# A state space branch rewritten: rotations on one engine, copies on two, 32-column output products

## The chip, the cores and the metric

The kernel runs on one core of one Trainium2 chip. The metric is the device time of one execution in microseconds (us). The core has five engines with a queue each: PE (TensorE, matrix products), DVE (VectorE), ACT (ScalarE), POOL (GpSimd) and SP, which here issues the weight transfers. Each works off its own queue in order and waits for the others by semaphores.

## What is computed

Two layers, 256 tokens of width 1024. Each layer is a feed-forward block, a mixer, and a second feed-forward block. The mixer projects the tokens to the input `u` of a state space branch, to an attention branch and to two gates, and adds up the gated branches:

```
h = rms_norm(x, norm_mix[l])
u, q_raw, k_cmp, ..., gate_a, gate_b = split(h @ w_in[l])
y_a = s5_branch(u, ...)              # 32 groups of 16 channels, 64 complex states each
y_b = nsa_branch(q_raw, ...) @ nsa_w_up[l]
x = x + (sigmoid(gate_a) * y_a + sigmoid(gate_b) * y_b) @ w_out[l]
```

and inside the state space branch

```
st[t] = abar * st[t-1] + bbar @ u[t]          (complex, per group)
y = gelu(Re(C st) + d * u)
val, gate = split(y @ w_glu); y_a = val * sigmoid(gate)
```

## The kernel before

**Weight stream and gemms.** All weights come as a stream of chunks. Each chunk is split into a rounded part on ACT (`whi`, line 156, or `hi` in line 318) and a rest on DVE (`wlo`, lines 157 and 318), with four buffers of each. A gemm multiplies two token tiles by four chunks: per k tile three products, lines 350 (`whi`, rounded activations), 351 (`whi`, their rest) and 352 (`wlo`), 512 columns each, 48 products in a gemm of `w_in`. The mixer's gemms follow each other: `u` (512 columns), keys and compressed values (384, then 408 columns), the compression products (line 488, 128x45), `q`, two gemms for each gate (called A0, A1, B0, B1 here), the GLU (four gemms), the up projection, the output.

**The state space branch** (`s5_main`) is a generator whose steps are issued between the chunks of these gemms. Four tokens make one chunk of the scan. Its steps: `U4`, 16 copies that put the four token phases of `uT` on four partition groups (u=0 on ACT, line 818; u=1 on DVE, line 820; u=2 and 3 on POOL through `gcopy`, line 480); 64 input products into banks `ya` and `yb` (line 488); a forward rotation by cos and sin (`rotate`; products on DVE, the additions of it on POOL in lines 881 and 885); two scans on DVE (line 838); a rotation back in two halves (half of the products, lines 882 and 883, and the subtraction of line 881 on POOL); the output products (line 488 once more) into `yb`: for each of 16 group pairs and each of three matrices (`K` on `U4`, two `C` on the states) two products of 64 output columns; and 32 gelus of 32x128 (line 857) that move the results from rows (token phase, channel) to rows of channels in `yt`, every fourth float of it at a time.

**Who stands near it.** On ACT, lines 1234 and 1236 (results of the 384 gemm, transposed by PE in line 1239), line 962 to 966 (408 gemm), line 1040 (gelu of the compressed keys `hid`, which needs `pb`, a one-column copy on DVE in line 1039), line 991 (the `q` gemm out of its bank) and 1264 (gates out of their banks). On DVE, lines 946 to 957 (rope of the keys) and 1008 to 1018 (of `q`), line 1048 (`kb`, which PE transposes in line 1055). The attention of each query tile goes by heads: scores on PE (line 1136), maximum on DVE, exponentials on ACT (1143), scaling on POOL (1159), transposes on PE (1169), copies on ACT (1171), products on PE (1180).

**What sets the order.** The instructions are written in the generator's order, but a scheduler in the build, with its own idea of durations, decides in which order each engine's queue gets them. So the change moves instructions that it doesn't name.

Of the kernel before, what the change touches and what calls it, by code (L numbers as in the profile page):

```python
# [24 lines left out]
# column offsets of the shape-only constants, packed side by side on 128 partitions  # L25
# [49 lines left out]
class Model:  # L75
# [31 lines left out]
    def add(k, ap, split=True, g=None):  # L107
        """g: (norm, first k tile) whose gains scale the rows"""
        k.chunks.append((ap, split, g))
# [65 lines left out]
    def next(k, la=None):  # L175
        """the next chunk of the stream; prepares later ones as far as buffers allow"""
        i = k.nu
        k.nu += 1
        if i and not k.chunks[i - 1][1]:
            k.held -= 1  # L180
        k.prepare(k.opt['LA'] if la is None else la)
        k.pull()
        return k.hl.pop(i)
# [132 lines left out]
    def split(k, src, hi, lo):  # L316
        """hi: src rounded to the product's type, lo: the rest"""
        return k.nc.scalar.copy(hi, src), k.nc.vector.tensor_sub(lo, src, hi.bitcast(F32))  # L318

    def rsqrt(k, ss, n, scale):  # L320
        """(ss*scale + eps)^-0.5 on [P, n]"""
# [13 lines left out]
    def norms(k):  # L335
        """1/rms of both token tiles, behind the weight preparation issued so far"""
# [3 lines left out]
    def transp4(k, src, t, half):  # L340
        """four 128x128 transposes of token-major src [128, 512] into hh/hl"""
# [12 lines left out]
    def finish(k, ys, sc, norm, parts):  # L354
        """x += sc * y and its transposed copy for the next phase. parts: the last products of token tile 0,
        and those of token tile 1 in two portions"""
# [24 lines left out]
    def gemm(k, stat, nk, cols, order=None, per=2, la=None):  # L381
        """two token tiles against the next weight chunks; returns the two banks.
        order: chunks per turn of a tile where the turns are to be kept"""
# [98 lines left out]
    def mm_cols(k, out, pairs, first, last=True):  # L482
        """sum of lhsT.T @ rhs over pairs, as two column tiles of the array that run side by side"""
# [8 lines left out]
    def s5_load(k, l):  # L492
        """DMAs of the S5 parameters of layer l"""
# [30 lines left out]
    def cmul(k, o, a, b, tmp, cost, M=None, conj=False):  # L524
        """(o0 + i o1) = (a0 +- i a1)(b0 + i b1), products on engine M; tmp(): scratch"""
# [18 lines left out]
    def s5_scalars(k):  # L544
# [31 lines left out]
        # angle to [-pi, pi]  # L576
# [19 lines left out]
        # expm1(a) = 2t/(1-t), cos-1 = -2 sin^2(th/2)  # L596
# [62 lines left out]
        # mag^4 and the unit rotation to the fourth power  # L659
# [11 lines left out]
    def s5_tables(k):  # L671
        """cos, sin of j*phi [128, 16, 64] and the decay of the scan"""
# [46 lines left out]
    def s5_mats(k):  # L719
# [7 lines left out]
        # powers times Bbar, dense: X[(g2 n), p, tau, c], tau = 3 - power  # L727
# [5 lines left out]
        # C transposed, pair-diagonal: CT[(g2 n), p, (g2' c)]  # L733
# [14 lines left out]
        # pair-diagonal copies, then the end-of-chunk input matrices  # L748
# [16 lines left out]
        # lag matrices: rows (tau, g2', c') hold lag 3 - tau  # L765
# [32 lines left out]
        # state-to-output matrices with abar^(s+1)  # L798
# [8 lines left out]
    def s5_main(k, uT):  # L807
        """uT [128 channels, 4, 256] -> yT hi/lo [128 channels, 4, 256]"""
# [4 lines left out]
        for q in range(4):  # L813
            for u in range(4):
                o = U4[u * 32:(u + 1) * 32].rearrange("p (a q) j -> p q a j", q=4)[:, q]
                i = uT[q * 32:(q + 1) * 32].rearrange("p a (j u) -> p u a j", u=4)[:, u]
                if u == 0:
                    S.copy(o, i)
                elif u == 1:
                    V.tensor_copy(o, i)  # L820
                else:
                    k.gcopy(o, i)
        yield 1.5
        yield 0.5
# [21 lines left out]
        yt = r4().rearrange("p (a t s) -> p a t s", a=4, s=4)  # L846
        for h in range(2):
            bk = k.bank((128, 8, 64), 'yb')
            for q in range(8):
                p = h * 8 + q  # L850
                k.mm_cols(bk[:, q], [(P['K'][:, p], U4[:, p]), (P['C'][0][:, p], Sp[0][:, p]),
                                     (P['C'][1][:, p], Sp[1][:, p])], q == 0)
# [522 lines left out]
```

## Time and profile before

| | |
|---|---|
| median of 3 runs | 1202.55 us (1201.87 to 1202.59) |
| span of the profiled execution | 1202.1 us |
| PE busy | 1162.6 us, 97% of the span |
| DVE / ACT / POOL busy | 844.5 / 687.7 / 251.4 us |
| PE idle between 220 and 350 us (first mixer), four longest waits | 5.3, 1.3, 1.2 and 0.5 us |
| the same between 810 and 940 us (second mixer) | 5.3, 1.2, 1.1 and 0.5 us |

An engine's busy time is the time covered by its instructions; PE's ends are modelled, and its products are pipelined, so what stands between two products is read from their starts. The span is a little shorter than the timed execution: the profiled one took 1202.1 us from first to last instruction, the median of the timed ones is 0.45 us longer. In a timeline row stand the start, the time covered, the engine, the line, the tiles written and read, the number of instructions merged, and in brackets the idle time ahead of it with the engine and line that ended it. An unqualified product of two f32 operands shows as two instructions, so 96 of them are 192 records.

### The profile page before, as it was taken

The numbers are of one execution on the slowest core, as the hardware profiler recorded it, in microseconds if no ns is written. First come the engines' busy times: TensorE is split into PE (matmuls) and PEld (weight loads), VectorE is DVE, ScalarE is ACT, GpSimd is POOL, SyncE is SP. The second block draws the span as 40 slices with busy tenths as digits, with TensorE's granted clock in tenths as the row PEclk, the third lists the DMA queues.
The fourth block names the chain that finished last, engine by engine and source line by source line (L and its number), as shares of the span: only waits on it lengthen the run. The fifth ranks groups of instructions, "written<-read, shape, count | busy, mean of one in ns | idle before, by whom it ended". The sixth has DMA issues, their size and how long they took to land. (4 is left out here: it accounts for less than half of the span.)

```text
span 1202.1 us, 18057 instructions
## 1 busy us (share of the span) xinstructions
PE 1162.6 (97%) x6326; PEld 947.3 (79%) x6326; DVE 844.5 (70%) x1466; ACT 687.7 (57%) x1228; POOL 251.4 (21%) x320
## 2 busy tenths in 40 slices
PE   7999999989999999999999999999899999999998
PEld 6888777877777888888888887778677778888886
DVE  5797979686865765555667987986967765655554
ACT  6655554738855565555566555555597645655552
POOL 3002654273212000000020053815532110000000
PEclk9999999999999999999999999999899999999999
DMA  7766555453543566656666656455635535666662
GB/s 234 220 182 186 166 156 183 116 158 112 178 126 98 175 210 185 186 182 187 189 183 183 196 160 181 140 155 147 193 89 158 132 117 172 210 179 189 192 183 80
DMA packets 150076, 200.44 MB, mean 167 GB/s; under 512 B 9952, under 2 KB 120832, under 8 KB 149984
## 3 DMA queue, kind: packets, MB, share of 16 engines
q1 hardware_dynamic: 148848, 197.46, 54.0%
q0 software_dynamic: 1136, 1.82, 0.9%
q8 instruction: 50, 0.82, 0.3%
q14 instruction: 42, 0.34, 0.1%
HBM read 198.18 MB, written 1.05 MB: 166 GB/s over the span
## 5 line engine op out<-in xcount | busy, mean ns | idle before, releaser
L157 DVE SCALAR_TENSOR_TENSOR wlo<-raw,gcol,whi 128x512 fp32r<-128x512 f32 (+2 forms) x480 | 363.6, 797 | 104.8 <-ACT whi L156 102.3
L156 ACT ACTIVATE whi<-raw,gcol 128x512 fp32r<-128x512 f32 (+2 forms) x480 | 315.0, 710 | 174.4 <-PE gu L351 78.0
L350 PE MATMUL gu<-whi,hh 128*128 128x512 f32 (+2 forms) x960 | 380.9, 397 | 13.0 <-ACT whi L156 10.6
L352 PE MATMUL gu<-wlo,hh 128*128 128x512 f32 (+2 forms) x960 | 376.1, 395 | 0.0
L351 PE MATMUL gu<-whi,hl 128*128 128x512 f32 (+2 forms) x960 | 375.9, 392 | 0.0
L318 DVE TENSOR_TENSOR wlo<-raw,whi 128x1024 fp32r<-128x1024 f32 x128 | 162.7, 1276 | 109.3 <-ACT whi L318 104.5
L350 PEld LDWEIGHTS gu<-whi,hh 128*128 128x128 f32 x960 | 181.9, 189 | 48.5 <-ACT whi L156 10.8
L318 ACT CAST whi<-raw 128x1024 fp32r<-128x1024 f32 x128 | 134.6, 1054 | 138.2 <-PE gu L351 123.0
L351 PEld LDWEIGHTS gu<-whi,hl 128*128 128x128 f32 x960 | 181.9, 190 | 35.7
L352 PEld LDWEIGHTS gu<-wlo,hh 128*128 128x128 f32 x960 | 181.5, 189 | 35.7 <-DVE wlo L157 0.2
L325 POOL TENSOR_SCALAR rs<-ss 128x1 f32<-128x1 f32 (+3 forms) x22 | 6.6, 301 | 388.7 <-ACT w2k L332 356.0
L351 PE MATMUL yb<-whi,w1k 128*128 128x512 f32 x176 | 71.5, 406 | 0.7 <-DVE w1k L318 0.7
L352 PE MATMUL yb<-wlo,w1k 128*128 128x512 f32 x176 | 69.1, 393 | 0.0
L350 PE MATMUL yb<-whi,w1k 128*128 128x512 f32 x176 | 69.0, 395 | 0.0
L351 PE MATMUL ya<-whi,w1k 128*128 128x512 f32 x176 | 68.8, 391 | 0.0
L352 PE MATMUL ya<-wlo,w1k 128*128 128x512 f32 x176 | 68.7, 390 | 0.0
L350 PE MATMUL ya<-whi,w1k 128*128 128x512 f32 x176 | 68.2, 393 | 0.0
L318 ACT CAST w1k<-tr 128x256 fp32r<-128x256 f32 x88 | 32.4, 369 | 46.3 <-PE tr L434 46.2
L1159 POOL TENSOR_SCALAR w2k<-w2k,sm 128x128 f32<-128x128 f32 (+1 forms) x64 | 33.8, 546 | 109.3 <-ACT w2k L1143 92.4
L451 DVE SCALAR_TENSOR_TENSOR w1k<-gu,rs,w1k 128x256 f32<-128x256 f32 x88 | 41.9, 478 | 20.1 <-ACT w1k L450 20.1
L450 ACT ACTIVATE w1k<-gu,rs 128x256 f32<-128x256 f32 x88 | 40.8, 466 | 21.7 <-PE gu L352 16.8
L318 DVE TENSOR_TENSOR w1k<-tr,w1k 128x256 fp32r<-128x256 f32 x88 | 36.7, 418 | 10.4 <-ACT w1k L318 10.3
(307 smaller groups left out, 1511.2 us busy)
## 6 DMA issues: line engine op xcount, KB each, us to landing
raw<-in_ffn_wi_dram SPq DMA_DIRECT2D x352, 256.0 KB, 3.3
raw<-in_ffn_wo_dram SPq DMA_DIRECT2D x88, 512.0 KB, 3.7
raw<-in_w_in_dram SPq DMA_DIRECT2D x48, 512.0 KB, 4.5
raw<-in_ssm_w_glu_dram SPq DMA_DIRECT2D x32, 256.0 KB, 3.3
raw<-in_w_out_dram SPq DMA_DIRECT2D x16, 512.0 KB, 3.9
raw<-in_cmp_w_dram SPq DMA_DIRECT2D x8, 512.0 KB, 5.5
raw<-in_nsa_w_up_dram SPq DMA_DIRECT2D x16, 256.0 KB, 4.2
raw<-in_w_in_dram SPq DMA_DIRECT2D x8, 408.0 KB, 4.1
```

The source lines that it names most:

```text
L156: k.hi_ins[i] = k.nc.scalar.activation(hi[:, s], r[:, s], AF.Copy, scale=c)
L157: k.nc.vector.scalar_tensor_tensor(lo[:, s], r[:, s], c, hi[:, s].bitcast(F32), op0=ALU.mult, op1=ALU.subtract)
L318: return k.nc.scalar.copy(hi, src), k.nc.vector.tensor_sub(lo, src, hi.bitcast(F32))
L325: k.nc.gpsimd.tensor_scalar(a, ss, scale, EPS, op0=ALU.mult, op1=ALU.add)
L350: mm(ps, a[0], b[0], start=first, stop=False)
L351: mm(ps, a[1], b[0], start=False, stop=False)
L352: return mm(ps, a[0], b[1], start=False, stop=last)
L450: m = nc.scalar.activation(sg, ps[t][:, :256], AF.Silu, scale=r[t])
L451: nc.vector.scalar_tensor_tensor(a, ps[t][:, 256:], r[t], sg, op0=ALU.mult, op1=ALU.mult)
L1159: G.tensor_scalar(w[:, i], p[:, i], cf[:, j:j + 1], 0.0, op0=ALU.mult, op1=ALU.add)
```

## The change

All of it is in `s5_main` and `rotate`; comments went too, so lines behind stand two or three lines earlier in the changed file (1234 is 1232 there, 838 is 835).

```diff
@@ s5_main: U4
-                if u == 0:
+                if u % 2 == 0:
                     S.copy(o, i)
-                elif u == 1:
+                else:
                     V.tensor_copy(o, i)
-                else:
-                    k.gcopy(o, i)
-        yield 1.5
-        yield 0.5
+            yield 0.7
@@ s5_main: output
+        T = ((P['K'], U4), (P['C'][0], Sp[0]), (P['C'][1], Sp[1]))
         for h in range(2):
-            bk = k.bank((128, 8, 64), 'yb')
-            for q in range(8):
-                p = h * 8 + q
-                k.mm_cols(bk[:, q], [(P['K'][:, p], U4[:, p]), (P['C'][0][:, p], Sp[0][:, p]),
-                                     (P['C'][1][:, p], Sp[1][:, p])], q == 0)
-                if q % 4 == 3:
-                    yield 0.9
-            for s in range(4):
-                for pq in range(4):
-                    S.activation(yt[pq * 32:(pq + 1) * 32, h * 2:h * 2 + 2, :, s],
-                                 bk[s * 32:(s + 1) * 32, pq:8:4, :], AF.Gelu_apprx_tanh)
-            yield 1.2
+            bk = k.bank((128, 2, 4, 64), 'yb')
+            for i, (m, v) in enumerate(T):
+                for a in range(2):
+                    for s in range(4):
+                        for q in range(4):
+                            p = h * 8 + a * 4 + q
+                            nc.tensor.matmul(bk[q * 32:(q + 1) * 32, a, s], m[:, p, s * 32:(s + 1) * 32], v[:, p],
+                                             start=(i == 0 and a == 0 and s == 0), stop=(i == 2),
+                                             skip_group_check=True)
+                    yield 0.4
+            S.activation(yt[:, h * 2:h * 2 + 2].rearrange("p a t s -> p a s t"), bk, AF.Gelu_apprx_tanh)
+            yield 0.6
@@ rotate
-        G = k.nc.gpsimd
-        add, sub = (G.tensor_add, G.tensor_sub) if first else (G.tensor_sub, V.tensor_add)
-        M = V if first else G
+        add, sub = (V.tensor_add, V.tensor_sub) if first else (V.tensor_sub, V.tensor_add)
         V.tensor_mul(t[0], xr, c)
         V.tensor_mul(t[1], xi, s)
         yield 1.2
         add(out[0][:, sl, oj], t[0], t[1])
-        M.tensor_mul(t[2], xi, c)
-        M.tensor_mul(t[3], xr, s)
-        yield 1.2 if first else 0.4
+        yield 0.6
+        V.tensor_mul(t[2], xi, c)
+        V.tensor_mul(t[3], xr, s)
+        yield 1.2
         sub(out[1][:, sl, oj], t[2], t[3])
-        yield 0.2 if first else 0.6
+        yield 0.6
```

The output products become 192 a layer instead of 96, each with 32 output columns, so that a result lies at once in the partitions of its channels, and two gelus of 128x512 a layer replace the 32.

Where the queues change, at the three places that the prediction speaks of. ACT, from the copies of `uT` out of its bank to the results of the 384 gemm (`r_2330` is `U4`, `kp` the keys); before:

```order
L1227 COPY r_2303<-tr 128x4x128 x2
L818 COPY r_2330<-r_2303 32x4x64 x4
L156 ACTIVATE whi<-raw,gcol 128x408 x6
L1234 ACTIVATE w1k<-gu,rs 128x256
L1236 ACTIVATE kp<-gu,rs 128x128
```

and in the changed kernel:

```order
L1225 COPY r_2303<-tr 128x4x128 x2
L818 COPY r_2330<-r_2303 32x4x64 x6
L156 ACTIVATE whi<-raw,gcol 128x408 x2
L818 COPY r_2330<-r_2303 32x4x64 x2
L156 ACTIVATE whi<-raw,gcol 128x408 x4
L1232 ACTIVATE w1k<-gu,rs 128x256
```

The last two of the eight copies now stand behind two weight casts, and line 1234 (1232) behind all eight.

DVE, from the end of the forward rotation to the second `pb` (`r_2387` and `r_2388` are the scanned states, `r_689` and `r_690` cos and sin; the scans show as SCALAR_TENSOR_TENSOR here); before:

```order
L883 TENSOR_TENSOR w2k<-yb,r_690 128x512
L838 SCALAR_TENSOR_TENSOR r_2387<-r_691,r_2387 128x1024
L838 SCALAR_TENSOR_TENSOR r_2388<-r_691,r_2388 128x1024
L878 TENSOR_TENSOR w2k<-r_2387,r_689 128x8x63
L967 TENSOR_SCALAR gate<-gate 128x24
L946 TENSOR_REDUCE ss_2598<-w1k 128x4
L879 TENSOR_TENSOR w2k<-r_2388,r_690 128x8x63
L878 TENSOR_TENSOR w2k<-r_2387,r_689 128x8x63
L879 TENSOR_TENSOR w2k<-r_2388,r_690 128x8x63
L967 TENSOR_SCALAR gate<-gate 128x24
L1039 COPY pb<-ya 128x1
```

and in the changed kernel:

```order
L881 TENSOR_TENSOR w2k<-yb,r_690 128x512
L878 TENSOR_TENSOR r_2387<-w2k 128x512
L947 TENSOR_TENSOR w1k<-kp,rs 128x256
L883 TENSOR_TENSOR r_2388<-w2k 128x512
L1037 COPY pb<-ya 128x1
L835 SCALAR_TENSOR_TENSOR r_2387<-r_691,r_2387 128x1024
L949 TENSOR_TENSOR w1k<-w1k,cg 128x256
L835 SCALAR_TENSOR_TENSOR r_2388<-r_691,r_2388 128x1024
L157 SCALAR_TENSOR_TENSOR wlo<-raw,gcol,whi 128x512
L875 TENSOR_TENSOR w2k<-r_2387,r_689 128x8x63
L955 TENSOR_TENSOR w1k<-w1k 128x256
L1037 COPY pb<-ya 128x1
```

The first `pb` now stands ahead of the scans, and the `q` gemm's first `wlo` behind both; the second half of the forward rotation (and so the scans) has moved behind both `gate` rows, and most of the rotation back to a place behind the rope of `q`.

PE, around the 408 gemm's end and the `q` gemm's first products (`ya<-kc` are the compression products); before:

```order
L352 MATMUL gu<-wlo,hh 128x408
L488 MATMUL ya<-kc_1836,raw 64x45 x64
L488 MATMUL yb<-r_2330,r_1662 64x64 x4
L350 MATMUL gu<-whi,hh 128x512
L351 MATMUL gu<-whi,hl 128x512
```

and in the changed kernel:

```order
L352 MATMUL gu<-wlo,hh 128x408
L488 MATMUL yb<-r_2330,r_1467 64x64 x15
L488 MATMUL ya<-kc_1836,raw 64x45 x64
L853 MATMUL yb<-r_2330,r_1662 32x64 x9
L350 MATMUL gu<-whi,hh 128x512
L351 MATMUL gu<-whi,hl 128x512
L350 MATMUL gu<-whi,hh 128x512
L351 MATMUL gu<-whi,hl 128x512
L853 MATMUL yb<-r_2330,r_1662 32x64 x26
L352 MATMUL gu<-wlo,hh 128x512
```

Fifteen of the input products have moved behind the 408 gemm, and 35 of the new output products stand ahead of the first product that needs `wlo`. The last 96 output products of a layer stand in one piece near the end of gemm B0, where before all 96 but one were done when gate gemm A1 began.

## Rows read from the trace of the kernel before

**Rows 1.** The page: engines' busy us (share of span), instructions; line 157's busy us, mean ns.

```profile
PE 1162.6 (97%) x6326; PEld 947.3 (79%) x6326; DVE 844.5 (70%) x1466; ACT 687.7 (57%) x1228; POOL 251.4 (21%) x320
...
L157 DVE SCALAR_TENSOR_TENSOR wlo<-raw,gcol,whi 128x512 fp32r<-128x512 f32 (+2 forms) x480 | 363.6, 797 | 104.8 <-ACT whi L156 102.3
```

**Rows 2.** Waits of PE, 220 to 350 us: waiting line, releaser, total us, times, longest.

```profile
PE gu L350 <- ACT whi L156: 5.3, 1, 5.3
PE gu L350 <- ACT r L1264: 1.3, 1, 1.3
...
PE tr L1055 <- DVE kb L1048: 0.5, 1, 0.5
```

**Rows 3.** Busy time by stretch: us, then per engine, granted clock, DMA share, GB/s.

```profile
261.00:264.20 3.20, 3.20 (x8) 2.60 (x9) 3.20 (x4) 3.20 (x7) 3.20 (x4) 0.54 0.00 0
```

**Rows 4.** Timeline of the copies of U4 and what follows on ACT.

```profile
229.69 2.63 ACT L818 COPY r<-r 32x256 f32<-32x256 f32 x4
232.35 3.27 ACT L156 ACTIVATE whi<-raw,gcol 128x408 fp32r<-128x408 f32 x6
235.52 0.45 ACT L1234 ACTIVATE w1k<-gu,rs 128x256 f32<-128x256 f32 x1
...
229.69 0.38 DVE L820 COPY r<-r 32x256 f32<-32x256 f32 x1 [3.87 <-ACT r L1227]
...
229.81 6.62 POOL L480 TENSOR_SCALAR r<-r 32x256 f32<-32x256 f32 x8 [6.78 <-ACT r L1227]
```

**Rows 5.** Timeline of PE: products with 64 output columns and their neighbours.

```profile
236.49 1.39 PE L488 MATMUL ya<-r,r 128*64 128x64 f32 x40 [1.21 <-POOL r L480]
...
249.90 5.58 PE L488 MATMUL ya<-kc,raw 128*64 128x45 f32 x128
255.29 0.42 PE L488 MATMUL yb<-r,r 128*64 128x64 f32 x8
...
274.42 0.34 PE L488 MATMUL yb<-r,r 128*64 128x64 f32 x4
274.68 0.44 PE L977 MATMUL tr<-id,w1k 128*128 128x128 f32 x2
275.05 0.92 PE L488 MATMUL yb<-r,r 128*64 128x64 f32 x24
275.90 0.50 PE L350 MATMUL gu<-whi,hh 128*128 128x512 f32 x1
276.24 0.39 PE L351 MATMUL gu<-whi,hl 128*128 128x512 f32 x1
276.47 0.39 PE L352 MATMUL gu<-wlo,hh 128*128 128x512 f32 x1
```

**Rows 6.** Timeline of DVE around the rotation back.

```profile
252.97 0.65 DVE L878 TENSOR_TENSOR w2k<-r,r 128x504 f32<-128x504 f32 x1
...
258.14 1.73 DVE L879 TENSOR_TENSOR w2k<-r,r 128x504 f32<-128x504 f32 x1
...
259.87 0.14 DVE L1039 COPY pb<-ya 128x1 f32<-128x1 f32 x1
```

**Rows 7.** Line 838 alone: the scans, shortest, median and longest in ns.

```profile
L838 DVE TENSOR_TENSOR_SCAN r<-r,r x4: 2258/2810/3361, 247.5 to 843.4; 128x1024 f32<-128x1024 f32 x4
```

**Rows 8.** Timeline of PE: products with 32 output columns while parameters are prepared.

```profile
750.29 1.10 PE L771 MATMUL tr<-r,w2k 128*32 128x64 f32 x64
751.32 0.44 PE L434 MATMUL tr<-id,w1k 128*128 128x128 f32 x2
```

**Rows 9.** Timeline of ACT: half of a layer's gelus.

```profile
297.80 6.45 ACT L857 ACTIVATE r<-yb 32x128 f32<-32x128 f32 x16
```

**Rows 10.** Timeline of PE and POOL: last head's scores, scaling and first transposes.

```profile
364.74 1.09 PE L1136 MATMUL ya<-kT,qT 128*128 128x512 f32 x4
...
379.10 0.60 PE L1169 MATMUL tr<-id,w2k 128*128 128x128 f32 x4
...
370.61 5.84 POOL L1159 TENSOR_SCALAR w2k<-w2k,sm 128x256 f32<-128x256 f32 x8 [6.04 <-ACT w2k L1143]
```

## The prediction

> **What bounds the kernel now.** I read the page first: PE is busy for 97% of the span [rows 1], so the time is PE's work plus PE's waits, and another engine matters only where PE waits for it. The table of PE's waits, by stretches, then shows where that is: around the state space branch in each mixer. In the first, one wait of 5.3 us for a weight cast and one of 1.3 us for a gate's way out of its bank [rows 2], and one of 1.21 us for POOL's copies of `u` [rows 5]. The second mixer repeats them within 0.2 us. The timeline tells why. The cast stands in ACT's queue behind the gelu of line 1040, that one waits for `pb`, and `pb` stands on DVE behind the rotation back and runs at 259.87 [rows 6]. DVE is that late because a product of the rotation takes 0.65 us when it begins alone and 1.73 us beside POOL's half of it [rows 6]. The wait for the bank has the gelus on ACT ahead of it, 16 of them in 6.45 us [rows 9].
>
> [...]
>
> So what this branch costs PE in a layer beyond its own products is 5.3 + 1.5 + 1.3 = 8.1 us, and the 1.21 us at the copies.
>
> **The change part by part, for one layer.** Times are those of the first mixer; the work of both is the same.
>
> *Copies of u.* POOL's eight end at 229.81 + 6.62 = 236.43 [rows 4]. DVE's first took 0.38 us, before POOL began; eight at that price end at 233 and delay nothing. ACT's take 2.63 / 4 = 0.66 us. By its new queue six end at 233.7, two casts of 3.27 / 6 = 0.55 us follow [rows 4], and the last copy ends at 236.1: three tenths of a us earlier than POOL's, no more. Line 1234, which ended at 235.97, now comes behind four more casts and ends at 236.1 + 4 x 0.55 + 0.45 = 238.7, and PE needs it for a transpose ahead of the 408 gemm. So PE waits until 236.2 for the copies, does 29 products, waits 0.8 us for line 1234 and comes to the gemm 1.2 us later than before. For this it has 16 instead of 20 input products left over, and these stand in two places instead of four between the gemm's products. What a place costs: 4 records take 274.68 - 274.42 = 0.26 us and 24 take 0.85 [rows 5], so 0.03 us a record and 0.14 us a run; the product behind a run takes 276.24 - 275.90 = 0.34 us against 0.23 for the next [rows 5]. That is 0.25 us a run, 0.06 us a product; four products and two or three runs are 0.9 to 1.0 us. Sum of this part: **+0.1 us**, bounds -1.2 (no wait is left) and +1.5.
>
> *Rotations and the way to the q gemm.* The forward rotation's second half now follows the 408 gemm's end at about 250.0: PE does 15 input products (to 251.0), DVE three products and two additions, a row of the keys between them: six steps of 0.6 us, the 0.65 without its tail, to 254.5. Then `pb`, so that the gelu of line 1040 and the first cast come at 256.1 and no longer wait; then two scans, 2.26 to 3.36 us each [rows 7]. I take the low end for both, since no POOL work of more than some instructions is left beside them: 259.3, and with 0.7 for a `wlo` (0.8 in the mean [rows 1]) the first of them at 260.0. PE does the compression products behind the 15 (255.29 - 249.90 = 5.4 us [rows 5], to 256.4), 35 output products and four gemm products, to 258.7. So it waits 1.3 us, and about 1.0 us more for the second `wlo`, which stands behind a rotation step, a row of the keys and the second `pb`: **2.3 us** in place of 5.3 + 1.5. Bounds: 0, if DVE starts 2.3 us earlier, and 4.8: scans at the median of 2.81 give 2.4 + 1.0, and the low clock may come back at 1.4.
>
> *The rest of the rotation back* (5 to 7 steps of 0.6 us) now lies on DVE in gate gemm B0. What hides it: PE's 48 products of a gate gemm take 48 x 0.23 = 11 us, in which DVE owes 8 `wlo`, 6.4 us at the mean, so there is room for it. Without the cover it would cost its 4 us; I take 0.
>
> *Output products.* 96 x 2 records of 64 columns are 192 x 0.03 = 5.7 us. The form of the new ones is in the trace: line 771, 32 columns of weights, 64 moved, four places in turn. 64 records take 751.32 - 750.29 = 1.03 us [rows 8]; less the 0.14 of a run that is 0.014 us a record, so 384 are 5.3 us. They stand in 13 runs against 9. 4 x 0.25 - 0.4 = **+0.6 us**; without the four runs it would be -0.4, and if the four places don't overlap at all it is +5.8.
>
> [...]
>
> *Gelus.* 12.9 us of ACT a layer [rows 9] become two instructions; a gelu of 32x128 takes 0.4 us, one of four times the columns between that and 1.6. On the path only the 1.3 us wait for the bank is in this, and it goes: by the new order nothing stands ahead of line 1264 there.
>
> *What is late next.* With all this PE ends gate gemm A0 some us earlier, and the chain of the compressed keys (POOL's root, rope, `kb`) is not shortened by as much; PE waited 0.5 us for it [rows 2], and by the same walk through the queues it waits 0.9 us more: **+0.9 us**, bounds 0 and 2.
>
> *Attention.* It begins about 10 us of gemm later in PE's order and ends at the same place. For the last head there were 379.10 - 364.74 = 14.4 us between scores and transposes; now 12 + 12 gemm products (5.5 us) stand there and some four groups of transposes, 0.6 us each [rows 10], with their products, about 9.6 us together. The scaling on POOL was done 370.61 + 5.84 - 364.74 = 11.7 us after the scores [rows 10], its first half some 3 us sooner. I put **+1.0 us** for what PE waits there, bounds 0 and 6 (two heads late by 3 us each).
>
> Sum: 8.1 - (0.1 + 2.3 + 0.6 + 0.9 + 1.0) = 3.2 us a layer, 6.4 for two. From the span of 1202.1 that is 1195.7; the median lies 0.45 us above the profiled span: **1196.2 us**.
>
> **The rivals.**
>
> *The wait only moves (within 0.2%).* DVE's chain to the first `wlo` takes the upper price, 4.8 instead of 2.3, and the `kb` wait is 1 us longer still. For it: the scans and the forward rotation are still one chain on one engine, now begun later. Against: `pb` no longer stands in it. 3.2 - 3.5 = -0.3 a layer: about 1203; with only the first half of it, 1201.
>
> *Attention becomes the bound (slower).* The place is from B1 to the up projection, the price what PE waits for line 1159. From 4.2 us a layer the gain is gone. At the bound of 6 it is 3.2 - 5 = -1.8 a layer: 1206.2. For it: 14.4 us of cover become 9.6. Against: ACT loses 10 us of gelus, and POOL all else.
>
> [...]
>
> *Nearly all waits go (faster still).* If `kb` and attention cost nothing and the first `wlo` comes 1 us sooner: 8.1 - 2.0 = 6.1 a layer, 1190.4. For it: DVE loses POOL beside it everywhere, and I counted that in one place.
>
> **How the numbers follow.** Forecast 0.48, only moved 0.19, attention 0.15, no overlap 0.05, nearly all 0.13. A measurement of this kernel tells 0.2%, 2.4 us, from no change. Faster by that are nearly all of the forecast (0.46), the largest gain (0.13) and a quarter of "only moved" (0.04): 0.63. Within are most of "only moved" and 0.03 of the rest: 0.17. Slower: 0.20, attention, no overlap and a little of the moved wait. The range reaches from the largest gain to the two slower cases' lower ends, 1190.4 to 1205.
>
> **What would show it.** Right: PE's 5.3 us wait is gone and less than 3 us stand in its place, the granted clock behind it is near 1; line 1264's wait is gone; the run of 96 products takes about 2.8 us; `pb` runs before the scans. [...]

## The result and the profile after

| | before | after |
|---|---|---|
| median | 1202.57 us (1201.87 to 1202.72) | 1189.15 us (1188.54 to 1189.75) |
| span of the profiled execution | 1202.1 us | 1187.7 us |
| PE busy in it | 1162.6 us | 1157.4 us |
| the rest of the span | 39.5 us | 30.3 us |

The ratio is 0.9891, 95% interval 0.9879 to 0.9903: 13.4 us less, where 6.4 were forecast (1196.2, range 1190.4 to 1205.0). The direction was right, the size was not, and the time lies below the range. The profiled executions differ by 14.4 us, of which 5.2 are PE's busy time and 9.2 are not.

The page of the changed kernel, engines' busy time (us, share of the span, instructions), against [rows 1]:

```profile
PE 1157.4 (97%) x6710; PEld 944.1 (79%) x6710; DVE 840.5 (71%) x1494; ACT 674.7 (57%) x1176; POOL 232.2 (20%) x284
```

PE's waits in the first mixer after the change, 220 to 350 us (waiting line, releaser, total us, times, longest):

```profile
PE ya L488 <- ACT r L818: 1.6, 1, 1.6
PE tr L1053 <- DVE kb L1046: 1.6, 1, 1.6
PE gu L352 <- DVE wlo L157: 1.5, 1, 1.5
PE tr L1237 <- ACT w1k L1232: 0.5, 1, 0.5
PE tr L994 <- DVE w2k L1016: 0.2, 1, 0.2
```

And in the kernel before, the rest of the view of which [rows 2] shows three lines:

```profile
PE ya L488 <- POOL r L480: 1.2, 1, 1.2
PE tr L1169 <- POOL w2k L1159: 0.8, 2, 0.5
...
PE ya L1079 <- DVE qT L318: 0.5, 1, 0.5
PE tr L1043 <- PE yb L488: 0.3, 1, 0.3
```

The first mixer's waits fall from 9.9 to 5.4 us. The 5.3 for the cast and the 1.3 for the gate's bank are gone, 1.5 stand in the `q` gemm. What the prediction did not have: the waits of the attention (lines 1169 and 1079) are gone too. In the second mixer they fall from 9.4 to 6.1. One of them has no counterpart in the kernel before:

```profile
PE yb L853 <- issue: 1.0, 1, 1.0
```

Behind the wait in the `q` gemm of the first mixer PE now runs at full speed; the stretch that answers to [rows 3] (us, PE busy, granted clock, DMA share, GB/s):

```profile
259.25:262.40 3.15, 3.15 (x34) 1.00 0.25 40
```

In the second mixer the half clock has not gone, it has moved. Before, it stood behind the wait in the `q` gemm, and longer than in the first mixer:

```profile
853.58:858.06 4.48, 4.48 (x11) 0.52 0.11 13
```

In the changed kernel it stands behind the 1.6 us for `kb`, which PE waits there as in the first mixer (until 873.4):

```profile
874.57:877.98 3.41, 3.41 (x10) 0.52 0.83 262
```

Between 261.5 and 263.5 and between 854.0 and 857.4 us before, and between 875.0 and 877.0 after, the granted clock is 0.50. PE was busy at it for 7.3 us in the two mixers before and for 3.4 us after. Products of a gemm start 0.43 us apart there (854.17, 854.60) and 0.23 us apart behind it (858.43, 858.66). I count half of such time as lost, an estimate from the clock.

DVE on the way to the first `wlo` of the `q` gemm, which answers to [rows 6] (start, us, line, tiles, idle before):

```profile
248.68 0.18 DVE L965 TENSOR_SCALAR gate<-gate 128x24 f32<-128x24 f32 x1 [3.64 <-ACT gate L964]
...
249.92 0.69 DVE L876 TENSOR_TENSOR w2k<-yb,r 128x512 f32<-128x512 f32 x1
...
253.26 0.15 DVE L1037 COPY pb<-ya 128x1 f32<-128x1 f32 x1
253.33 2.48 DVE L835 TENSOR_TENSOR_SCAN r<-r,r 128x1024 f32<-128x1024 f32 x1
255.73 0.62 DVE L949 TENSOR_TENSOR w1k<-w1k,cg 128x256 f32<-128x256 f32 x1
256.27 2.28 DVE L835 TENSOR_TENSOR_SCAN r<-r,r 128x1024 f32<-128x1024 f32 x1
258.47 0.72 DVE L157 SCALAR_TENSOR_TENSOR wlo<-raw,gcol,whi 128x512 fp32r<-128x512 f32 x1
```

Two things are to be seen. `pb` runs ahead of the scans, at 253.3 instead of 259.9. And ahead of 248.7 DVE stands still for 3.64 us. The last 15 input products, which the second half of the forward rotation needs, now stand on PE behind the 408 gemm, from 248.74 on, and `L876` follows them at 249.92. The credits in the new code (explained below) turned out to cost half as much as the whole change won; that this idle time is the reason, the runs below do not bear out.

### The profile page after: what moved, and what is told of

It is laid out like the page before. It is cut to its first block, busy times and chain, and to the rows that moved or that the text cites. A ratio compares the mean times of both kernels' runs of the same rounds, so it can differ in the third digit from the quotient of the medians.

```text
span 1187.7 us, 18769 instructions
## 1 busy us (share of the span) xinstructions
PE 1157.4 (97%) x6710; PEld 944.1 (79%) x6710; DVE 840.5 (71%) x1494; ACT 674.7 (57%) x1176; POOL 232.2 (20%) x284
## 4 chain that ended last, share of the span: by engine, by line
PE 89%; POOL 3%; DVE 3%; ACT 2%; issue 2%; DMA 1%; SPq 0%; DVEq 0%; ACTq 0%
PE gu L352 19%; PE gu L350 19%; PE gu L351 19%; PE ya L352 4%; PE yb L350 4%; PE ya L350 4%; PE yb L352 4%; PE yb L351 4%; PE ya L351 4%; POOL r L480 2%; PE tr L434 2%; PE yb L1178 1%; DVE wlo L157 1%; PE tr L344 1%; PE tr L1167 1%
## 5 line engine op out<-in xcount | busy, mean ns | idle before, releaser
L157 DVE SCALAR_TENSOR_TENSOR wlo<-raw,gcol,whi 128x512 fp32r<-128x512 f32 (+2 forms) x480 | 359.0, 786 | 111.0 <-ACT whi L156 108.5
L1157 POOL TENSOR_SCALAR w2k<-w2k,sm 128x128 f32<-128x128 f32 (+1 forms) x64 | 38.9, 629 | 99.8 <-ACT w2k L1141 62.8
L318 DVE TENSOR_TENSOR w1k<-tr,w1k 128x256 fp32r<-128x256 f32 x88 | 36.7, 419 | 10.3 <-ACT w1k L318 10.2
```

What stands on the lines that cost most here:

```text
L157: k.nc.vector.scalar_tensor_tensor(lo[:, s], r[:, s], c, hi[:, s].bitcast(F32), op0=ALU.mult, op1=ALU.subtract)
L1157: G.tensor_scalar(w[:, i], p[:, i], cf[:, j:j + 1], 0.0, op0=ALU.mult, op1=ALU.add)
```

## The experiments

Behind each `yield` of the branch stands a number, its credit: a gemm hands out 1.0 at every weight chunk that it takes, and the branch goes on until that is spent. So the numbers, too, place the branch's instructions between others, and the change altered them with the engines: 4 x 0.7 for 1.5 + 0.5 at the copies, 3.6 in all for 2.6 (forward) and 2.2 (back) in a rotation. Below, "the copies", "the rotations" and "the output" are the three parts with their credits, unless something else is said. Each time is a median, the ratio is to the kernel before on the same chip.

### One part alone

Each run takes one piece of the diff shown ahead. `r_only` takes that in `rotate`:

```diff
-        M = V if first else G
...
-        M.tensor_mul(t[2], xi, c)
+        V.tensor_mul(t[2], xi, c)
...
```

`c_only` takes that at `U4`, and `o_only` that at the output products and gelus:

```diff
-                if u == 0:
+                if u % 2 == 0:
...
+            yield 0.7
```

```diff
-            bk = k.bank((128, 8, 64), 'yb')
+            bk = k.bank((128, 2, 4, 64), 'yb')
...
+            S.activation(yt[:, h * 2:h * 2 + 2].rearrange("p a t s -> p a s t"), bk, AF.Gelu_apprx_tanh)
```

> The kernel before, with the rotations of the new kernel (all eight steps on DVE, and the credits that the new code yields between them). Theory A, engine: the 5.3 us that PE waited in the q gemm, and the 1.5 us of half clock behind them, hang on the rotations alone. DVE's queue now has pb behind both scans and ahead of the rotation back: the second half of the forward rotation ends at about 248.4, the scans (2.3 us each without POOL beside them) at 255.0, pb follows, then four products of 0.6 us and a key row, and the first wlo is there at 258.7 instead of 262.2. PE waits some 2.5 us instead of 5.3 and comes back at full speed: 2.8 + 1.5 = 4.3 us a layer less, about 1194. Theory B, pace: the order that the credits give counts more than the engine, and pb has to stand ahead of the scans, which it does only together with the new copies: r_only then wins less than 2 us a layer, 1199 or more.

Measured: 1203.79 us, ratio 1.0020 (1.0011 to 1.0029): slower. Waits of PE, 220 to 350 us, with the rotations alone:

```profile
PE gu L350 <- ACT r L1263: 4.1, 1, 4.1
PE gu L352 <- DVE wlo L157: 2.4, 1, 2.4
PE tr L1054 <- DVE kb L1047: 1.6, 1, 1.6
...
PE gu L350 <- ACT whi L156: 0.6, 1, 0.6
```

The wait in the `q` gemm is 3.0 us (0.6 for the cast and 2.4), near the 2.5 of theory A, though the half clock behind it stayed. But more than that gain is given back further on. ACT there (start, us, line, tiles, count):

```profile
314.67 6.38 ACT L857 ACTIVATE r<-yb 32x128 f32<-32x128 f32 x16
321.08 0.69 ACT L1263 ACTIVATE r<-gu,rh 128x512 f32<-128x512 f32 x1
```

The rotations moved the branch's second half later (before, these sixteen gelus ran at 297.80 [rows 9]), and its sixteen gelus now stand on ACT right ahead of the instruction that clears a bank for PE. In the kernel before the first half's sixteen stood so, at 1.3 us; here it is 4.1. Behind it the clock falls too (columns as above):

```profile
321.78:327.50 5.72, 5.68 (x15) 0.56 0.27 89
```

In the two mixers PE is busy at a granted clock of 0.50 for 19.1 us, where it was 7.3. That is 5.9 us lost, more than the 1.1 by which the waits grew; PE's work at full clock became 5.0 us shorter.

> The kernel before, with only the copies of u changed (half on ACT, half on DVE, and 0.7 of credit behind each group of four). Theory A: PE's wait for the copies goes from 1.2 to 1.6 us, five input runs become fewer, the wait in the q gemm stays 5 us or more since POOL still does half of the rotation: 1202.6 within 2 us. Theory B: the new credits put the forward rotation and the scans behind the 408 gemm, which with POOL in the rotation makes the chain end later: 2 to 4 us a layer slower, 1207 to 1210.

Measured: 1213.55 us, ratio 1.0099 (1.0084 to 1.0114): slower by 12 us, the way of theory B, but by more than its 5 to 8. PE waits 1.7 and 4.9 us in the `q` gemm, where it was 5.3; that is the later chain. What theory B did not have is larger: 4.2 us a mixer in the attention for ACT (line 1140), and 16.7 us at a granted clock of 0.50 for 7.3.

> The kernel before, with only the output products 32 columns wide and the two gelus. Theory A: PE's wait of 1.3 and 1.1 us for the gate's bank goes (16 gelus of 0.4 us no longer stand ahead of it on ACT), the products cost the same 15 us in all (384 records of 41 ns before, 768 of about 20 ns now): 2.4 us for both layers, 1200.2. A further 1.3 us a layer if the small waits of the attention (0.51, 0.51 and 0.33 us) hang on the same gelus: 1197.6. Rival: those small waits went because the attention comes later in the order, which only the other parts do: 1200 or more.

Measured: 1195.79 us, ratio 0.9953 (0.9940 to 0.9965). All of PE's waits in the first mixer, 220 to 350 us:

```profile
PE gu L350 <- ACT whi L156: 5.1, 1, 5.1
PE ya L488 <- POOL r L480: 1.2, 1, 1.2
```

Every wait behind the `q` gemm is gone, the bank's as well as those of `kb` and the attention: 1.3 + 0.8 + 0.5 + 0.5 + 0.3 = 3.4 us here and 1.1 + 0.8 + 0.5 + 0.5 = 2.9 in the second mixer, which is the gain of 5.9 and a little more. PE's busy time is 1163.3 us for 1162.6, with 10.6 us of it at a granted clock of 0.50 for 7.3. At full clock it is 0.9 us less: the products themselves cost nothing.

### All but one part

`no_c`, `no_o` and `no_r` are the changed kernel with one of these three pieces undone.

> The new kernel with the copies of u as before (POOL's eight and the old credits): rotations and output products are new. Chain theory: with the rotations alone PE waited 4.1 and 4.5 us for the gate's bank behind sixteen gelus, and with one gelu in their place that goes; 2.4 + 0.6 us at the q gemm and 1.6 at the kb rows stay. 1203.8 - 2 x 4.6 = 1194.6 or a little less. Rival, the parts add up: 1201.7 + 2.1 - 5.9 = 1197.9. Rival, the copies give nothing here: the time of the new kernel, 1189.

Measured: 1182.18 us, ratio 0.9833 (0.9817 to 0.9849). By the ratios this is 7 us **faster than the changed kernel**; none of the three expectations had it.

> The new kernel with the output products and the 32 gelus as before: copies and rotations are new. Chain theory: the second half of the gelus again stands on ACT ahead of the line that clears the gate's bank, as with the rotations alone, 4.1 to 4.5 us a layer, and the q gemm has the new kernel's 1.5: 1189.2 + 2 x 4.4 = 1198. Rival, the parts add up: 1201.7 + 2.1 + 11.9 = 1215.7. Rival, the bank costs the 1.3 us that it cost in the kernel before: 1192.

Measured: 1208.19 us, ratio 1.0050 (1.0035 to 1.0065). The mechanism expected is there, at twice the price; ACT in the first mixer:

```profile
310.45 12.85 ACT L854 ACTIVATE r<-yb 32x128 f32<-32x128 f32 x32 [1.50 <-PE yb L488]
```

All 32 gelus of the layer in one row, and the gate's bank behind them: PE waits 6.8 us for it in one place, 9.3 in three.

> The new kernel with the rotations as before, half on POOL: copies and output are new. If the copies cost the same 7 to 12 us wherever they are put: 1195.8 + 7 to 12 = 1203 to 1208. Chain theory: in the run with the copies alone PE waited 4.9 and 1.7 us in the q gemm behind DVE, 1.9 us for the gate's bank and 4.2 us in the attention for ACT; with one gelu in place of sixteen the last two go, and the rest stays, 1213.5 - 2 x 6 = 1201.5. Rival, the rotations matter little: 1189 to 1192.

Measured: 1200.14 us, ratio 0.9988 (0.9979 to 0.9997), near the chain theory. PE waits 1.5 and 4.3 us in the `q` gemm, and nowhere for a gelu.

With these the eight combinations are complete (ratio to the kernel before):

| | old output | new output |
|---|---|---|
| neither | 1 | 0.9953 |
| copies | 1.0099 | 0.9988 |
| rotations | 1.0020 | **0.9833** |
| both | 1.0050 | 0.9891 |

No part has a price of its own. The rotations lose 2 us without the new output and win 0.9953 - 0.9833 = 1.2%, 14 us, with it; the output wins 6 us alone and 22 on top of the rotations; the copies lose in each of the four pairs, 12, 4, 4 and 7 us.

Part of this is the clock. PE's busy time at a granted clock of 0.50 in the two mixers (us, half of it lost by the estimate above):

| | old output | new output |
|---|---|---|
| neither | 7.3 | 10.6 |
| copies | 16.7 | 8.0 |
| rotations | 19.1 | 0 |
| both | 17.6 | 3.4 |

So of the 16 us between the rotations' loss without the new output and their gain with it, (19.1 - 7.3) / 2 + 10.6 / 2 = 11.2 are the clock: with the old output it comes down behind the `q` gemm's wait and behind the one for the sixteen gelus in both mixers, and once behind `kb`; with the new output nowhere.

### The copies: engine or credits

> The new kernel, but with 2.0 of credit behind all sixteen copies of u, as before, instead of 0.7 behind each group of four. The copies stay on ACT and DVE, the rotations keep the new credits. With the copies as before the time was 1182, with the new ones 1189. Theory credits: the seven us are the order that the credits give, which keeps half of the forward rotation behind the 408 gemm on DVE, where it stands idle for 3.6 us in the new kernel: with the old credits 1182 to 1184. Theory engines: they are ACT's share of the copies (1.6 us of PE's wait instead of 1.2, and what stands behind them on ACT): 1187 to 1190.

```diff
                 else:
                     V.tensor_copy(o, i)
-            yield 0.7
+        yield 1.5
+        yield 0.5
```

Measured: 1182.65 us, ratio 0.9841 (0.9828 to 0.9855).

> The other way round: the new kernel with POOL's eight copies as before, but with the new credits at them. Theory credits: 1188 to 1190, as the new kernel. Theory engines: 1182 to 1184, as with the copies before.

```diff
                 else:
                     k.gcopy(o, i)
-        yield 1.5
-        yield 0.5
+            yield 0.7
```

Measured: 1188.53 us, ratio 0.9888 (0.9875 to 0.9902). The four corners are clean: old credits 1182.2 and 1182.7, new credits 1188.5 and 1189.2, whichever engine copies. The seven us are the order. What in it costs them is only partly seen. In the changed kernel DVE stood still for 3.64 us ahead of 248.7. DVE in `no_c` on the same stretch:

```profile
243.96 0.69 DVE L878 TENSOR_TENSOR w2k<-yb,r 128x512 f32<-128x512 f32 x1 [1.44 <-PE yb L488]
247.12 0.69 DVE L879 TENSOR_TENSOR w2k<-yb,r 128x512 f32<-128x512 f32 x1 [2.47 <-PE yb L488]
...
249.53 0.69 DVE L886 TENSOR_TENSOR r<-w2k 128x512 f32<-128x512 f32 x1
```

The forward rotation ends at 250.2 instead of 253.3. But DVE waits as long here, 1.44 + 2.47 us for input products, and PE's wait in the `q` gemm is no shorter (1.6 us for 1.5). So nothing here shows that the idle time of DVE is what the credits cost.

The profiles of the changed kernel and of `c_oldcred` differ by 7.5 us: 2.4 are idle time of PE (mainly: the wait for `kb` is 0.8 instead of 1.6 in each mixer, and the 1.0 called issue is gone), 5.1 are busy time (1157.4 and 1152.3 us). Of these 1.7 are the clock: neither run with the old credits comes down to 0.50 in its mixers, both with the new credits do, for 3.4 us in the second mixer. The other 3.4 are open. `no_c_newcred` and `no_c` differ by 6.7 us in the same way: 3.2 are idle time, 2.0 of them again called issue, 1.7 the clock, right behind that, and 1.8 are open. PE's timeline has the 384 records of a layer's output products in 11 runs of 3 to 128 with the old credits and in the changed kernel in 15 runs of 2 to 192. The waits called issue come up only in the longest of these, at 192 (on them see the last section). That the number of runs is what makes PE busier was not tried apart.

### The rotations: engine or credits

> The kernel before with the output products and gelus of the new one (195.8 above 1000 with those alone), its rotations still half on POOL, but with the new credits in the rotations. It tells whether the 13.6 us that the rotations won on top of the output (1195.8 to 1182.2) are the engine or the credits. Engine: POOL's half still doubles DVE's products beside it (1.5 to 1.7 us for 0.65), PE still waits 3 to 5 us in the q gemm, and the time is 1193 or more. Credits: the order is that of the run at 1182, and so is the time, within 3 us.

```diff
         add(out[0][:, sl, oj], t[0], t[1])
+        yield 0.6
...
-        yield 1.2 if first else 0.4
+        yield 1.2
...
-        yield 0.2 if first else 0.6
+        yield 0.6
```

Measured: 1202.7 us, ratio 1.0006 (0.9997 to 1.0014), no faster than the kernel before. DVE there:

```profile
254.52 0.14 DVE L1042 COPY pb<-ya 128x1 f32<-128x1 f32 x1
...
258.44 1.74 DVE L157 SCALAR_TENSOR_TENSOR wlo<-raw,gcol,whi 128x512 fp32r<-128x512 f32 x1
```

`pb` is early here, at 254.5; what is late is DVE's own work, since a `wlo` beside POOL's half of the rotation takes 1.74 us where it takes 0.72 without, and a row of the keys 1.57. So 4.4 us of waits stay in the `q` gemm, as the engine theory had it. They are less than the 5.1 of `o_only`, though; that the run is 7 us slower than that one lies further on, in a wait of the attention that `o_only` does not have (350 to 400 us, and again in the second mixer):

```profile
PE tr L1172 <- ACT w2k L1174: 1.9, 1, 1.9
```

and in the clock, 15.0 us of busy time at a granted clock of 0.50 for 10.6.

> The same from the other side: copies as before, output new, rotations on DVE, but with the old credits in the rotations. Engine: 1182 to 1186 (with the new copies the old credits in the rotations cost 2.4 us). Credits: 1193 or more, as with the output alone.

The edit is the reverse of the last one, in `no_c`.

Measured: 1184.06 us, ratio 0.9852 (0.9838 to 0.9866). Here it is the engine, from both sides: with either credits it wins 12 us or more. The credits alone cost 6 us beside POOL (0.9953 to 1.0006), and on DVE they change nothing clear of noise (0.9852 and 0.9833). The kernel before has such a slow `wlo` beside POOL too: the one at 262.26 takes 1.68 us while POOL does the subtractions of line 881 (260.00 to 263.39), and the one at 258.47 in the changed kernel, with the rotation on DVE, 0.72.

### The output: products or gelus

> The new output products alone (all else as before), but each of the two gelus cut into sixteen, 32 partitions by 128 columns as before, so that ACT has its 12.9 us of gelus a layer again. If the 5.9 us that the output part won alone hang on ACT's time for the gelus: PE's wait for the gate's bank (1.3 and 1.1 us) and the four small waits of the attention and of kb are back, and the time is that of the kernel before, 1200 to 1203. If they hang on the products (their places, their number, their banks): 1195 to 1197 as with two gelus.

```diff
-            S.activation(yt[:, h * 2:h * 2 + 2].rearrange("p a t s -> p a s t"), bk, AF.Gelu_apprx_tanh)
+            yo = yt[:, h * 2:h * 2 + 2].rearrange("p a t s -> p a s t")
+            for pq in range(4):
+                w = slice(pq * 32, (pq + 1) * 32)
+                for a in range(2):
+                    for s in (slice(0, 2), slice(2, 4)):
+                        S.activation(yo[w, a, s], bk[w, a, s], AF.Gelu_apprx_tanh)
```

Measured: 1198.12 us, ratio 0.9966 (0.9953 to 0.9979), between the two. The run doesn't do what it was meant to, for its gelus are cheaper (ACT):

```profile
280.78 2.17 ACT L865 ACTIVATE r<-yb 32x128 f32<-32x128 f32 x8 [0.57 <-PE yb L856]
```

One comes every 0.27 us instead of every 0.40 [rows 9], 8.7 us a layer instead of 12.9. Each reads and writes the same 32 partitions, where those before changed partitions on the way; that this is why is not shown. The bank's wait is 0.3 us, and those of `kb` and the attention stay away. So how much of the 3.4 us hangs on ACT's time and how much on where the new products stand is open.

### The cost of a 32-column product

> The new kernel with each output product issued twice into the same place, always four column places in turn, so that the output of the branch is doubled before its gelu: 384 records more in a layer. At 15 ns a record, as the run of 192 in 2.9 us says, 5.8 us a layer and 11.5 in all: 1200.7. [...]

```diff
-                    for s in range(4):
+                    for s, d in [(s, d) for s in range(4) for d in range(2)]:
...
-                                             start=(i == 0 and a == 0 and s == 0), stop=(i == 2),
+                                             start=(i == 0 and a == 0 and s == 0 and d == 0), stop=(i == 2 and d == 1),
```

Measured: 1209.0 us, ratio 1.0063 (1.0050 to 1.0076): 19.9 us above the changed kernel for 768 records, 26 ns each, where 15 were expected. But the records in a run stand closer. PE in the long run of the second half, first mixer:

```profile
309.24 2.43 PE L853 MATMUL yb<-r,r 128*32 128x64 f32 x159
313.05 1.99 PE L853 MATMUL yb<-r,r 128*32 128x64 f32 x128 [1.38 <-issue]
318.15 0.85 PE L853 MATMUL yb<-r,r 128*32 128x64 f32 x33 [3.11 <-issue]
```

159 records take 2.43 us and 128 take 1.99, 15 ns each. Between them PE waits for nothing that the profile shows, 4.5 us in this mixer and 2.4 in the second, which the views call issue. So 768 x 15 ns = 11.5 us are the records, and 6.9 for 1.0 in the changed kernel are stalls; the rest of the 19.9 is not placed. And the `wlo` product behind takes 0.80 us for 0.51: PE is back at the lower clock (0.62 granted from 318 to 320). This is also the second mixer's new wait of 1.0 us in the changed kernel:

```profile
897.05 2.55 PE L853 MATMUL yb<-r,r 128*32 128x64 f32 x166
900.59 0.61 PE L853 MATMUL yb<-r,r 128*32 128x64 f32 x26 [0.99 <-issue]
```

### The credits of the whole, and faster versions

> The new kernel with every operation on its new engine, but with the credits of the kernel before at the copies (2.0 behind all sixteen) and in the rotations (1.2, 1.2 and 0.2 forward, 1.2, 0.4 and 0.6 back). By the queue of DVE, pb then stands behind both scans and eight products of the rotation back. Theory A, engine: the rotations on DVE are what matters, the time stays within 2 us of the new kernel, 1187 to 1191. Theory B, pace: the first whi of the q gemm waits for that pb. Scans end at 254.9, eight products of 0.6 us and the key rows bring pb to 260.6 and the first wlo to 263, while PE is there at about 255.5: a wait of 7 us and the half clock behind it, 6 to 7.4 us a layer more than the new kernel, 1201 to 1204.

```diff
-            yield 0.7
+        yield 1.5
+        yield 0.5
...
-        yield 0.6
...
-        yield 1.2
+        yield 1.2 if first else 0.4
...
-        yield 0.6
+        yield 0.2 if first else 0.6
```

Measured: 1185.09 us, ratio 0.9862 (0.9849 to 0.9876), faster than the changed kernel. Both theories were wrong, B by its arithmetic: I let the forward rotation begin at the end of the 408 gemm, but with the old credits it runs beside that gemm. The scans end at 251.5, not 254.9, `pb` comes at 256.7, and PE waits 0.5 us for the `wlo` and, in the output products, 1.5 for the rotation back.

> The new kernel with the old credits (the last run of the first four), and of the sixteen copies of u twelve on DVE (0.38 us each) and four on ACT (0.66 us each). PE's waits there were 0.9 us for ACT's copies and 1.1 us for line 1232, which stands behind ACT's copies and casts. If ACT's copies are the cause: both waits fall by 1.5 us together a layer, some 3 us less than that run, 1182. Rival: DVE then has 4.6 us of copies ahead of its wlo for the 408 gemm, and PE waits for those instead: within 1 us of that run.

```diff
-                if u % 2 == 0:
+                if u == 0:
                     S.copy(o, i)
```

Measured: 1183.23 us, ratio 0.9838 (0.9824 to 0.9853). The two waits at the copies fall from 0.9 + 1.1 to 0.5.

> New output, rotations on DVE with the new credits, and of the copies of u twelve on DVE and four on ACT, with the old credits behind all sixteen. Of the 4.7 us that PE waits in a mixer when half of the copies are on ACT with these credits, 0.9 stand before ACT's copies and 1.1 before line 1233 behind them; twelve copies on DVE took 1.5 of these in the run with the old credits everywhere. If they do here: 1182.6 - 3 = 1179.6, less than any other. If DVE's wlo for the 408 gemm, now behind 4.6 us of copies, are late instead: 1182 to 1183.

The edit is that of `oldpace_dve`, in `c_oldcred`.

Measured: 1180.35 us, ratio 0.9815 (0.9803 to 0.9828), the lowest time of all, though its interval overlaps that of `no_c`: 22 us less than before, 9 less than the change. PE waits 3.0 us in the first mixer, 1.5 of them in the `q` gemm and 0.6 at the copies.

## Why the prediction was wrong, by its steps

All values for one layer, as the mean of the two mixers where they differ. The forecast gain was 3.2 us, the measured one 6.7. The step that failed most is the attention: it was to cost 1.0 us and won 1.3 to 1.4.

**What is removed, 8.1 us: 7.5.** The waits of 5.3 and 1.3 us (1.1 in the second mixer) are gone. The half clock is gone in the first mixer (granted 1.00) and stands behind `kb` in the second. It cost 3.6 us in both layers before and 1.7 after, so 1.0 a layer came back, not 1.5. The 1.5 in the 8.1 is 3.2 x (1 - 0.54), from [rows 3]. The prediction took the first mixer's row for both. One reading of it was wrong without harm: the sixteen gelus ahead of the bank's wait are those of the first half, at 280.7 to 288.0, not those of [rows 9].

**Copies, +0.1: -0.5.** The single times were right: ACT's first six copies took 3.96 us and the last ended at 236.1, line 1237's wait is 0.5. The two waits come to 2.1 us for 1.2. PE reaches the 408 gemm 1.4 us later, where 1.2 was forecast; first the row before, then the one after:

```profile
238.00 0.43 PE L350 MATMUL gu<-whi,hh 128*128 128x408 f32 x1
239.41 0.45 PE L350 MATMUL gu<-whi,hh 128*128 128x408 f32 x1
```

But from there to the compression products, at 249.90 before [rows 5] and 249.61 now, it takes 10.2 us instead of 11.9: fewer runs of input products saved 1.7 us, not the 0.9 to 1.0 of the prediction. And no input product is left for later, where four were. PE is 0.5 us ahead when the compression products are done (255.2 for 255.7). By the prediction's own figures the term would have been 1.2 less 0.9 to 1.0, so +0.2 or +0.3. What part of the new order comes from the credits alone I never asked. That is no term of this sum; the runs put 3.5 us a layer on it.

**Way to the `q` gemm, 2.3: measured 1.5 in the first mixer, 1.4 in the second.** The first wait, 1.3 in the prediction, is 1.5. The times around it were all about a us late: I let the 408 gemm end at 250.0, which held the input products left over, and then counted 15 of them once more. PE's row for them in the changed kernel:

```profile
248.74 1.09 PE L488 MATMUL yb<-r,r 128*64 128x64 f32 x29
```

So DVE's `L876` started at 249.92, and not at 251.0, and PE was as much earlier; the wait between them did not change by it. The chain behind it was right: `pb` ahead of the scans, scans of 2.28 to 2.48. What failed is the second wait, 1.0 us for the next `wlo`. DVE makes it from 260.12 on, and PE, which has output products and transposes to do before, comes to the products that read it at 261.90 without waiting:

```profile
260.12 0.73 DVE L157 SCALAR_TENSOR_TENSOR wlo<-raw,gcol,whi 128x512 fp32r<-128x512 f32 x1
261.90 0.74 PE L352 MATMUL gu<-wlo,hh 128*128 128x512 f32 x2
```

**Rest of the rotation, 0: right.** No wait stands there.

**Output products, +0.6: about 0, and 0.5 for the stall.** The records cost 15 ns, as line 771 had it [rows 8]:

```profile
310.75 2.89 PE L853 MATMUL yb<-r,r 128*32 128x64 f32 x192
```

With the output alone PE's busy time at full clock fell by 0.9 us for both layers, so the extra runs cost next to nothing. For the case "no overlap" in the chances, which also gives the upper end of the range, no run shows the price a record; the runs showed 15 ns. What I had no term for is the stall inside a long run, 1.0 us in the second mixer.

**Gelus: right**, 1.19 and 1.10 us each, between the 0.4 and 1.6 that I gave, and PE does not wait for their bank or the gate's.

**`kb`, 0.5 + 0.9: measured 1.6.** Right within 0.2; that the clock falls behind it in one mixer is the loss counted above.

**Attention, +1.0: wrong in sign, the largest miss.** Instead of a cost, the 0.8 + 0.5 us that the attention already lost were won (and in the first mixer 0.3 at line 1043, less 0.2 at line 994): 2.3 us off. I looked at the last head, where the change takes cover away, and not at the first ones, where the waits of before stood (lines 1079 and 1169 at 309.6 to 325 us), 5 to 20 us behind sixteen gelus on ACT [rows 9]. `o_only` shows that the output part alone removes them; whether by ACT's time or by the new places of the products is open.

**PE's own work.** PE's busy time fell by 2.6: 1.0 are the clock, 1.4 the input products above. The other 0.2 I can't place.

Together 3.2 - 0.6 + 0.6 + 0.9 + 0.1 - 0.2 + 2.3 + 0.2 = 6.5, near the 6.7. The largest of the rivals, "nearly all waits go", gave 6.1 and was nearest by its number, but not by its mechanism: `kb` costs more than it had, the attention less than nothing. The rivals of the other side did not occur: no wait as long as the one removed took its place in this combination. In others it did; the `r_only` and `no_o` runs are that rival, with the gelus in its place, which I had not named.

## What to carry over

Price the parts of a change in the combination in which they will run: here the same rotation lost 2 us or won 14, according to what stood on ACT behind it. Where a number in the code sets how much of a side branch is issued between other work, take it as a change of its own and vary it alone first: one such number cost half as much as the whole change won. Behind each wait that goes or comes read the granted clock as well, in every layer: here the clock made two thirds of the difference between the rotations' loss and their gain. When the waits of before are read for what goes, read also the small ones further on, and what stood ahead of them on the engine that the change relieves.

## What the runs showed of the hardware

In long runs of 32-column products PE stood still for 1.0 to 3.1 us where the profile shows nothing that it waited for. In the changed kernel the stall, 1.0 us, came 166 records into such a run, in `no_c_newcred` it took 2.0 us, in `dup_out` it came after 159 and 128 in the first mixer and after 241 in the second, while a run of 192 in the first mixer passed without. Behind the 241 of `dup_out`:

```profile
912.49 1.32 PE L853 MATMUL yb<-r,r 128*32 128x64 f32 x79 [1.36 <-issue]
...
914.87 0.86 PE L853 MATMUL yb<-r,r 128*32 128x64 f32 x45
916.77 0.53 PE L853 MATMUL yb<-r,r 128*32 128x64 f32 x19 [1.03 <-issue]
```

Between the two there are 79, then four gemm products, then 45: 128 records again, as between the two stalls of the first mixer. The trace of the changed kernel has one thing more: a 16 KiB packet on queue q8, which the page of the profile calls instruction, starts at 898.16 and takes 0.98 us, and the stall ends 1.45 us behind it, at 900.59. There are 52 such packets in the whole changed kernel, and PE's waits have no other stall of the kind. In `dup_out` three such packets fall between 300 and 322 us, where two stalls lie. What PE waits for there is not shown.

In these runs the clock behind a wait is not told by the wait's length alone. In the first mixer of the changed kernel 1.5 us in the `q` gemm and 1.6 at `kb`, 29 us later, left it at 1.00; in the second the same 1.6 at `kb`, 29 us behind a wait of 1.0, were followed by 3.4 us of 0.52. In `r_only` 2.4 us, with 0.6 shortly ahead, were followed by 0.62 (the mean of 259 to 263), as in the kernel before 5.3 us by 0.54 [rows 3] and, in the second mixer, by 4.5 us of 0.52. The stretch of `r_only`, columns as above:

```profile
259.00:263.00 4.00, 4.00 (x15) 0.62 0.41 119
```

So a wait of 2.4 us cost about the same 4.0 x 0.38 = 1.5 us on top as one of 5.3 in the first mixer.
